# Soft mixture of experts by Strassen products: the left operand of P6 kept in DRAM and used again for P3, and two inner products of seven P3 pairs split once more

## The chip, the cores and the metric

One NeuronCore of a Trainium2 chip runs the whole kernel in one launch. The metric is the device time of the execution in microseconds. The engines are TensorE (PE, with its weight loads PEld beside it), VectorE (DVE), ScalarE (ACT), GpSimd (POOL) and SyncE (SP). SP, ACT and POOL issue DMAs, each on a queue of its own: in the profile q1 carries SP's, q10 ACT's and q0 POOL's.

## What is computed

```python
probs = softmax(router_logits)                 # 16 x 512 tokens, 8 experts
for e in range(n_experts):                     # hidden 512, expert_hidden 2048
    output += probs[:, :, e:e+1] * np.matmul(x, expert_weights[e])
```

The sum over experts is one matrix product: the left operand has a row for each of 8192 tokens and a column for each pair of expert and hidden index (8 x 512 = 4096), with entries prob times x; the right operand is the stack of expert weights, 4096 x 2048.

## The kernel before

**Two levels of Strassen products.** The outer level (Winograd's form, seven products P1 to P7) halves the tokens of a block of 512 into a and b of 256 (16 such blocks, q = 0 to 15), the experts into 0 to 3 and 4 to 7, and the output columns into 1024 and 1024. Each outer product (`Product`, L538) is made by seven inner ones, the steps 1, 5, 6, 2, 7, 3, 4 (`STEPS`, L353), whose operands are halves of 128 tokens, two experts (8 chunks of 128) and 512 columns. A step is 8 matmuls of 128 x 128 by 128 x 512 (`step`, L546); after it `post` (L554) takes sums from PSUM to SBUF with ACT or DVE, and `sink` stores them. Operands are f16.

**Left operands** (`Left`, L443) are two tiles `z` of 128 x 2048, made by DVE in `make`: `times` multiplies the transposed block of x (`xT`) by probabilities spread over partitions (`pT`). With Xa, Xb the blocks and P1, P2, PQ the probabilities of the low experts, of the high ones and their sum, P5 uses Xb PQb; P6 uses `of` minus a product, Z6 = Xb PQb - Xa P1a; P7 and P3 use a difference of two products (`less`), each with a second product in the tile `u`. P3's is Xa PQa - Xb PQb. From a left operand come the difference `d` (step 6) and the sum for steps 3 and 7.

**Right operands** are seven tiles `w` of 1 MB, of 128 x 8 x 512. There are 15 buffers for `w`. P7, P4 and P3 find theirs in DRAM (`wd`) and fetch them on ACT's queue (`fetch_w`, L162; `turnover`, L1064): one tile at every third slot, from the stage before on.

**Stages.** A stage is a pair of products whose steps alternate (`run`, L796), a slot being one step; 14 slots make a pair. The order of stages is: P1 pairs, P2 with P1, P2 pairs, a P5 pair (`k5`), P6 with P5, P6 with P7 (`k7`), P4 with P7, P4 with P3 (`k3`), seven P3 pairs, and P3 of q = 15 alone. The calls registered by `at` run at the beginning of a slot. The lefts of the next stage are queued for DVE after the first slot (L809), the loads of the stage after that are begun there too, or later if `late` says so (L811). DVE's queued work is put between the evacuations by a planned clock of PE and DVE (`slack`, L384), and all engines keep the order in which the program records their instructions.

**The split of P1.** In three P1 pairs, inner products 1 and 5 of both instances are split once more (`by_thirds`, L733). The two instances share the right operand, so that their two left tiles form the two rows of a third 2 x 2 level; the chunks halve into 4 and 4, the columns into 256 and 256. Fourteen groups of 4 matmuls with 256 columns (L764) take the place of four steps of 8 with 512. `Thirds` (L488) makes four sums of the left tiles on DVE, into tiles `h`, and `third_sums` (L178) four sums of a right tile. Partial sums go through ACT copies (L767 to L771, L781) and DVE adds (L774, L777).

**Order on the DMA queues.** SP takes its DMAs in program order, and each waits on SP for what it needs: a buffer's last reader, a store's landing, or the DMA eight places earlier in the joint sequence of SP's and ACT's DMAs, since these share eight semaphores in turn. The same holds for ACT's DMAs, behind which ACT's copies stand. POOL stores results (`out_dram<-h`) and has eight semaphores of its own. SP also loads the sums that P6, P7 and P2 are built upon (`h<-kept`, `h<-out_dram`), and transposes x as it first comes in.

Of the kernel before, what the change touches and what calls it, by code (L numbers as in the profile page):

```python
# [31 lines left out]
def kernel(  # L32
# [41 lines left out]
    def h_tile(shape, dtype):  # L74
        return hpool.tile(shape, dtype, name="h", tag="h")
# [30 lines left out]
    def tt(o, a, b, op):  # L106
        dve(nc.vector.tensor_tensor(out=o, in0=a, in1=b, op=op))  # L107
# [9 lines left out]
    def sp(o, i):  # L117
        note(nc.sync.dma_start(out=o, in_=i))
# [15 lines left out]
    def new_w():  # L134
        return wpool.tile([P, K8, NB], f16, name="w", tag="w")
# [223 lines left out]
    class Task:  # L359


        def __init__(self, cost, make):
            self.cost, self.make, self.done = cost, make, False
# [31 lines left out]

    class XBlock:


        def __init__(self, h, tile_=None):
            self.h, self.t, self.xs, self.new = h, tile_, None, tile_ is not None  # L400
# [21 lines left out]

    class PBlock:


        def __init__(self, h, first, tile_=None):
            self.h, self.first, self.t = h, first, tile_
# [15 lines left out]
    class Left:  # L443


        def __init__(self, xb, pb, less=None, of=None):
            self.xb, self.pb, self.less, self.of = xb, pb, less, of
            self.t, self.task, self.s2, self.i = [None, None], {}, None, None

        def make(self, k):  # L450
            if self.of is not None:
                need(self.of.task[k])
            t = self.t[k] = new_z()
            times(t, k, self.xb, self.pb)
            if self.less is not None:
                u = new_u()
                times(u, k, *self.less)
                tt(t, t, u, SUB)
            if self.of is not None:
                tt(t, self.of.t[k], t, SUB)  # L460

        def queue_make(self, k):
            cost = 1.22 + (2.45 if self.less is not None else 0) + (1.23 if self.of is not None else 0)
            self.task[k] = later(cost, lambda: self.make(k))

        def queue_s2(self):
# [13 lines left out]
        def op(self, p):  # L480
# [4 lines left out]
                    3: (self.i, 0), 7: (self.i, 1)}[p]  # L485
            return t[:, :, ds(i * HP, HP)]

    class Thirds:  # L488


        def __init__(self, a, b):
            self.a, self.b, self.s, self.task = a, b, {}, None

        def make(self):
            e0, e1 = ds(0, C), ds(C, C)
            a, b = self.a.t[0], self.b.t[0]
            for p, x, y, op in ((5, b[:, e0], b[:, e1], ADD), (6, None, a[:, e0], SUB),
                                (3, a[:, e1], None, SUB), (7, a[:, e0], b[:, e0], SUB)):
                o = self.s[p] = h_tile([P, C, HQ], f16)
                x = self.s[5] if x is None else x  # L500
                y = self.s[6] if y is None else y
                tt(o, x, y, op)
# [119 lines left out]


    stages = []
    hooks, late = {}, {}

    def at(stage, slot, make):
        hooks.setdefault((stage, slot), []).append(make)
# [15 lines left out]
    def left_of(r, q, fresh=True):  # L644
        a, b = 2 * q, 2 * q + 1
        if r == 1:
            pt = PBlock(a, P1, xp1[q - 2][1] if q in (2, 3) else None)
            if q in (2, 3):
                xs[a] = XBlock(a, xp1[q - 2][0])
            return Left(xblock(a), pt), [xblock(a), pt]  # L650
        if r in (2, 4):
            h, pt = (a, PBlock(a, P2)) if r == 2 else (b, PBlock(b, P2))
            return Left(xblock(h), pt), [xblock(h), pt]
        if r == 5:
            pt = PBlock(b, PQ)
            return Left(xblock(b), pt), [xblock(b), pt]
        if r == 6:
            pt = PBlock(a, P1)
            return Left(xblock(a), pt, of=lefts[5, q]), [xblock(a), pt]
        pa, pb = PBlock(a, P1 if r == 7 else PQ), PBlock(b, P1 if r == 7 else PQ)  # L660
        return Left(xblock(a), pa, (xblock(b), pb)), [xblock(a), pa, xblock(b), pb]

    def kept_rows(q):
# [43 lines left out]
    def start_loads(stage):  # L707
        if stage < len(stages):
            for p in stages[stage]:
                for load in p.loads:  # L710
                    load.begin()

    def finish_loads(stage):
        if stage < len(stages):
# [18 lines left out]
    def by_thirds(stage):  # L733

        some = stages[stage]
        left = thirds[stage]
        cols = [ds(i * HQ, HQ) for i in range(2)]
        place, keep = {}, {}

        def at_once(what):  # L740
            if what not in place:
                t = place[what] = (bank2 if what[0] == "x" else bank)()
                if what[0] in "gh":
                    some["gh".index(what[0])].banks["x" if what[1] == 1 else "q"] = t
            return place[what]
        slot = 0
        for n, (p, r) in enumerate(((1, 1), (5, 1), (1, 5), (1, 6), (5, 6), (5, 5), (1, 2),
                                    (1, 7), (5, 7), (1, 3), (1, 4), (5, 2), (5, 3), (5, 4))):
            if n in (0, 4, 7, 11):
                for make in hooks.get((stage, slot), ()):  # L750
                    make()
                slot += 1
                if slot == 2:
                    queue_lefts(stage + 1)
                    start_loads(stage + 2)
            x = at_once(("x", p))[:, cols[0]]
            q = at_once("q")[:, cols[p // 5]] if n > 1 else None
            g = at_once(("g", p))
            if r == 1:
                keep[p] = half()  # L760
            o = q if r in (5, 3) else g[:, cols[0]] if r == 2 else x
            z, w = left.op(r, p // 5), third[p][r]
            for c in range(C):
                mm(o, z[:, c, :], w[:, c, :], (r == 1 or (p, r) == (1, 5)) and c == 0, c == C - 1)  # L764
            slack(0.4375, LAG if n < 6 else 1.3)
            if r == 1:
                act(nc.scalar.copy(g[:, cols[0]], x))  # L767
            elif r == 5:
                act(nc.scalar.copy(keep[p][:, cols[1]], q))
            elif r == 6:  # L770
                act(nc.scalar.copy(keep[p][:, cols[0]], x))  # L771
            elif r == 7:
                evacuated(0.42)
                tt(at_once(("h", p))[:, cols[1]], x, keep[p][:, cols[1]], ADD)  # L774
            elif r == 3:
                evacuated(0.42)
                tt(g[:, cols[1]], q, keep[p][:, cols[0]], ADD)  # L777
                if p == 1:
                    some[0].post(1)
            elif r == 4:  # L780
                act(nc.scalar.copy(place["h", p][:, cols[0]], x))  # L781
                if p == 1:
                    some[1].post(1)
        for product in some:
            product.post(5)
        return 4
# [9 lines left out]
    def run(stage):  # L796
        some = stages[stage]
        for p in some:
            p.left.queue_i()
        n = by_thirds(stage) if stage in thirds else 0  # L800
        for i in range(n // 2, len(some[0].steps)):
            for p in some:
                for make in hooks.get((stage, n), ()):
                    make()
                p.step(p.steps[i])
                slack()
                p.post(p.steps[i])
                n += 1
                if n == 1:  # L809
                    queue_lefts(stage + 1)  # L810
                if n == late.get(stage, 1):  # L811
                    start_loads(stage + 2)
                if n == 5:
                    store_loads(stage + 1)
                if n == 7:
                    finish_loads(stage + 2)
# [32 lines left out]
        add(product(3, q), product(3, q + 1))  # L849
    end = add(product(3, 15))  # L850
    late[k3 - 1] = 6
    products[4, 15].apart = True

    def claim(of, tn):
# [142 lines left out]
    def slots_after(stage, slot, n):  # L997
        slot += n
        while slot >= 7 * len(stages[stage]):
            slot -= 7 * len(stages[stage])  # L1000
            stage += 1
        return stage, slot
# [58 lines left out]

    RAW = {1: (0, 0), 2: (1, 0), 3: (1, 1)}

    def turnover(stage, place, r, raw):  # L1064

        right[r].w = {}

        def fetch(p):
            if p in RAW:
                right[r].w[p] = fetch_w(raw, RAW[p])  # L1070
            else:
                right[r].w[p] = fetch_w((r, p), (0, 0))
        at(stage - 1, 9, lambda: fetch(1))
        for i, p in enumerate(STEPS[1:]):
            at(*slots_after(stage, place + 1, 3 * i), lambda p=p: fetch(p))
    turnover(k7 - 1, 1, 7, "t3")
    turnover(k7, 0, 4, "t4")
    turnover(k3 - 1, 1, 3, "b22")


    finish = products[3, 15]
# [32 lines left out]
    finish.step, finish.post = step_at_end, post_at_end  # L1114

    for stage in range(1, ND):
        thirds[stage] = Thirds(*(p.left for p in stages[stage]))
    need_first = [right[1].task[p] for p in (6, 7, 4)]
    for p in (2, 3):
        lefts[1, p].queue_make(0)  # L1120
# [39 lines left out]
```

## Time and profile before

| | |
|---|---|
| median of 3 runs | 1373.86 us (1373.67 to 1374.54) |
| profiled execution: its own time, its span | 1374.01 us, 1372.3 us |
| PE busy in the span | 1365.2 us (99%) |
| DVE, ACT, POOL busy | 1125.6, 190.2, 411.3 us |
| granted clock of TensorE, mean | 0.999 |
| DMA | 338.03 MB, 246 GB/s over the span |
| z<-xT,pT 128x2048, mean of one | 1218 ns |
| stage k5 begins, k7, k3, first P3 pair | about 401, 776, 1163, 1187 us |

The span is the time from the first to the last instruction of the core; the execution has 1.7 us around it. The page lists busy time by engine, then the span in 40 slices, the DMA queues, the chain of work that ended last, and groups of instructions with their mean duration and what ended the idle time before them. Matmuls overlap in the pipeline, so the mean that a group shows for one (378 ns) is longer than the step from one to the next. The trace behind the page answers for any stretch which engine did what, and how long a DMA took from its issue to landing.

### The profile page before, as it was taken

The page shows a single profiled execution, that of the slowest core. Times are in us where ns is not written, and L with a number is a line of the kernel's source. Part 1 is how long each engine was busy: PE and PEld are TensorE (multiplying, and loading weights), DVE is VectorE, ACT ScalarE, POOL GpSimd, SP SyncE. Part 2 cuts the span into 40 slices and gives each one's busy share as a digit, 9 for nine tenths or more (in the row PEclk, how much of TensorE's full clock was granted, in tenths as well). Part 3 has the DMA queues.
Part 4 walks back from the last instruction along what each step waited for, and adds up shares of the span by engine and source line. Part 5 has one row for each costly group of instructions (what it writes and reads, how often), then busy time and mean ns, then how long its engine had stood idle before and what let it go on. Part 6 is the DMA issues. An engine that isn't in the chain of part 4 may idle for free.

```text
span 1372.3 us, 17676 instructions
## 1 busy us (share of the span) xinstructions
PE 1365.2 (99%) x6462; PEld 629.2 (46%) x6462; DVE 1125.6 (82%) x1322; ACT 190.2 (14%) x341; POOL 411.3 (30%) x652
## 2 busy tenths in 40 slices
PE   9999999999999999999999999999999999999998
PEld 4455444444444444444444444444444444444444
DVE  7877767679789888788887988889889898988882
ACT  3332111100011111111111100000000000222221
POOL 3223333331223342334332122333333322232332
PEclk9999999999999999999999999999999999999999
DMA  9998999999898998899897997988898979998786
GB/s 182 231 248 222 212 255 254 243 297 389 239 311 247 297 303 241 268 269 249 243 279 264 335 400 207 235 234 210 227 235 225 244 208 311 254 183 181 167 147 106
DMA packets 191272, 338.03 MB, mean 246 GB/s; under 512 B 52944, under 2 KB 86992, under 8 KB 187472
## 3 DMA queue, kind: packets, MB, share of 16 engines
q0 software_dynamic: 88688, 185.12, 55.9%
q1 hardware_dynamic: 98464, 123.34, 30.5%
q10 hardware_dynamic: 4032, 28.44, 5.3%
q8 instruction: 50, 0.82, 0.2%
q14 instruction: 38, 0.31, 0.1%
HBM read 207.65 MB, written 156.43 MB: 265 GB/s over the span
## 4 chain that ended last, share of the span: by engine, by line
PE 99%; DMA 1%; POOL 0%; issue 0%; ACT 0%; POOLq 0%
PE ps L130 71%; PE pt L130 28%; DMA w<-in_expert_weights_dram 1%; POOL w L121 0%; ACT h L1110 0%; POOL ident L225 0%; POOLq L225 0%; POOLq L1144 0%
## 5 line engine op out<-in xcount | busy, mean ns | idle before, releaser
L130 PEld LDWEIGHTS <-z 128*128 128x128 f16 x5392 | 527.5, 98 | 628.3 <-issue 1.2
L130 PE MATMUL ps<-w,z 128*128 128x512 f16 (+1 forms) x3648 | 804.7, 378 | 0.0
L121 POOL DMA_DIRECT2D out_dram<-h x380 | 248.7, 673 | 745.7 <-ACT h L588 371.2
L130 PE MATMUL pt<-w,z 128*128 128x512 f16 (+1 forms) x1744 | 392.7, 376 | 1.1 <-DMA w<-in_expert_weights_dram 1.1
L107 DVE TENSOR_TENSOR h<-ps,h 128x512 f32<-128x512 f32 x246 | 168.4, 688 | 128.9 <-PE ps L130 122.4
L107 DVE TENSOR_TENSOR z<-xT,pT 128x2048 f16<-128x2048 f16 x220 | 267.0, 1218 | 1.6 <-issue 0.8
L130 PE MATMUL ps<-w,d 128*128 128x512 f16 x880 | 199.1, 379 | 0.0
L107 DVE TENSOR_TENSOR h<-pt,h 128x512 f32<-128x512 f32 x169 | 115.6, 688 | 67.1 <-PE pt L130 62.5
L130 PEld LDWEIGHTS <-d 128*128 128x128 f16 x880 | 86.1, 98 | 103.2
L107 DVE TENSOR_TENSOR z<-z,d 128x2048 f16<-128x2048 f16 x110 | 132.4, 1217 | 0.0
L107 DVE TENSOR_TENSOR w<-w 128x1024 f16<-128x1024 f16 (+2 forms) x100 | 106.1, 1070 | 4.6 <-DMA wd<-w 2.9
L588 ACT COPY h<-ps 128x512 f32<-128x512 f32 x64 | 37.5, 586 | 486.0 <-PE ps L130 457.5
L575 ACT COPY h<-ps 128x512 f32<-128x512 f32 x90 | 52.7, 586 | 373.5 <-PE ps L130 334.5
L107 DVE TENSOR_TENSOR z<-z,u 128x2048 f16<-128x2048 f16 x64 | 78.4, 1225 | 2.2
L107 DVE TENSOR_TENSOR u<-xT,pT 128x2048 f16<-128x2048 f16 x64 | 78.0, 1219 | 0.0
L107 DVE TENSOR_TENSOR d<-z 128x1024 f16<-128x1024 f16 x110 | 75.1, 686 | 1.7
L107 DVE TENSOR_TENSOR ps<-ps,h 128x512 f32<-128x512 f32 (+1 forms) x72 | 48.0, 668 | 15.7 <-PE ps L130 15.2
L121 POOL DMA_DIRECT2D w<-in_expert_weights_dram x65 | 48.9, 784 | 34.0 <-DMA wd<-w 23.3
L121 POOL DMA_DIRECT2D wd<-w x86 | 48.2, 585 | 36.0 <-DVE w L107 25.6
L121 POOL DMA_DIRECT2D kept<-h x56 | 30.8, 550 | 71.4 <-ACT h L575 39.1
L107 DVE TENSOR_TENSOR h<-h 128x512 f32<-128x512 f32 (+2 forms) x69 | 45.1, 676 | 0.1
L567 ACT COPY ps<-ps 128x512 f32<-128x512 f32 x45 | 25.7, 570 | 114.6 <-PE ps L130 107.6
(66 smaller groups left out, 231.9 us busy)
## 6 DMA issues: line engine op xcount, KB each, us to landing
out_dram<-h POOLq DMA_DIRECT2D x380, 256.0 KB, 6.1
pT<-p_dram SPq DMA_DIRECT2D x140, 256.0 KB, 5.9
w<-wd ACTq DMA_DIRECT2D x27, 1024.0 KB, 9.2
h<-kept SPq DMA_DIRECT2D x100, 256.0 KB, 5.8
xT<-x SPq DMA_DIRECT2D x87, 256.0 KB, 5.7
wd<-w POOLq DMA_DIRECT2D x72, 256.0 KB, 5.6
w<-in_expert_weights_dram POOLq DMA_DIRECT2D x35, 512.0 KB, 10.5
h<-out_dram SPq DMA_DIRECT2D x68, 256.0 KB, 5.3
```

The lines of the kernel that those rows point to most:

```text
L107: dve(nc.vector.tensor_tensor(out=o, in0=a, in1=b, op=op))
L121: note(nc.gpsimd.dma_start(out=o, in_=i, **how))
L130: note(nc.tensor.matmul(ps, z, w, start=start, stop=stop, skip_group_check=True))
L567: act(nc.scalar.copy(self.banks["b"], x))
L575: act(nc.scalar.copy(o[TN[p]], b if p == 2 else x))
L588: act(nc.scalar.copy(o[tn], b))
```

## The change

With Xa PQa = Xa P1a + Xa P2a, the left operand of P3 is also Xa P2a - Z6. The change writes both tiles of each Z6 to DRAM (`z_dram`, 16 x 1 MB, two stores of 512 KB on SP per q, in the stage before P6 of that q and at the beginning of its stage), loads it as one tile `w` for P3 (`ZBlock`), and makes P3's left operand by one product and one subtraction (`kept`). The loads of block b for P3 go. The seven P3 pairs are then run by `by_thirds`, with sums of P3's right tiles 1 and 5 (`third3`, made in stage `k3`) and with the sums of left tiles in a buffer of `w` instead of `h` (`room`). P3's weights are fetched at every second slot (`every=2`), all within the stage `k3 - 1` and the first slot of `k3`; in stage `k3` the lefts of the next stage are queued after slot 7 and the loads of the first P3 blocks begin at slot 10, but for the kept tiles of q = 1 and 2, which are loaded at slots 0 and 2.

```diff
-        def __init__(self, xb, pb, less=None, of=None):
+        def __init__(self, xb, pb, less=None, of=None, kept=None):
...
+            if self.kept is not None:
+                tt(t, t, self.kept.t[:, ds(k * K8, K8), :], SUB)
...
+    class ZBlock:
...
+        def begin(self):
+            self.t = new_w().rearrange("p k (two t) -> p (k two) t", two=2)
+            sp(self.t, z_dram[self.q])
...
-        def __init__(self, a, b):
-            self.a, self.b, self.s, self.task = a, b, {}, None
+        def __init__(self, a, b, weights, room=None):
...
+            if self.room is not None:
+                t = self.room().rearrange("p (s c) (two t) -> p s c two t", s=2, two=2)
+                t = {p: t[:, i // 2, :, i % 2] for i, p in enumerate((5, 6, 3, 7))}
...
-        pa, pb = PBlock(a, P1 if r == 7 else PQ), PBlock(b, P1 if r == 7 else PQ)
+        if r == 3:
+            pt, kept_z = PBlock(a, P2), ZBlock(q)
+            return Left(xblock(a), pt, kept=kept_z), [xblock(a), pt, kept_z]
+        pa, pb = PBlock(a, P1), PBlock(b, P1)
...
-                if n == 1:
+                if n == wait_for.get(stage, 1):
                     queue_lefts(stage + 1)
...
+    late[k3] = 10
...
-        at(stage - 1, 9, lambda: fetch(1))
-        for i, p in enumerate(STEPS[1:]):
-            at(*slots_after(stage, place + 1, 3 * i), lambda p=p: fetch(p))
+        if every == 3:
+            at(stage - 1, 9, lambda: fetch(1))
+        for i, p in enumerate(STEPS[every == 3:]):
+            at(*slots_after(stage, place + 1, every * i), lambda p=p: fetch(p))
...
-    turnover(k3 - 1, 1, 3, "b22")
+    turnover(k3 - 1, 1, 3, "b22", 2)
+
+    for q in range(16):
+        z_dram[q] = dram.tile([P, 2 * K8, HQ], f16, name=f"z_{q}")
+
+        def keep_z(k, q=q):
+            sp(z_dram[q][:, ds(k * K8, K8), :], lefts[6, q].t[k])
+        k, half_way = k5 + 1 + q, 7 * len(stages[k5 + q]) * 9 // 14
+        at(k - 1, half_way, lambda keep_z=keep_z: keep_z(0))
+        at(k, 0, lambda keep_z=keep_z: keep_z(1))
...
+    at(k3, 0, load_z(1))
+    at(k3, 2, load_z(2))
...
+    def third_of_p3(p):
+        def make():
+            third3[p] = third_sums(right[3].w[p])
+        later(2.76, make)
+    at(k3, 3, lambda: third_of_p3(1))
+    at(k3, 5, lambda: third_of_p3(5))
+    wait_for[k3] = 7
...
     for stage in range(1, ND):
-        thirds[stage] = Thirds(*(p.left for p in stages[stage]))
+        thirds[stage] = Thirds(*(p.left for p in stages[stage]), third)
+    for stage in range(k3 + 1, end):
+        thirds[stage] = Thirds(*(p.left for p in stages[stage]), third3, new_w)
```

More of the change, by code (lines that the diff above doesn't have):

```diff
@@ L396 @@
     class XBlock:
+        by_hook = False
         def __init__(self, h, tile_=None):
@@ L423 @@
     class PBlock:
+        by_hook = False
         def __init__(self, h, first, tile_=None):
@@ L443 @@
     class Left:
-        def __init__(self, xb, pb, less=None, of=None):
-            self.xb, self.pb, self.less, self.of = xb, pb, less, of
+        def __init__(self, xb, pb, less=None, of=None, kept=None):
+            self.xb, self.pb, self.less, self.of, self.kept = xb, pb, less, of, kept
             self.t, self.task, self.s2, self.i = [None, None], {}, None, None
@@ L460, in make @@
                 tt(t, self.of.t[k], t, SUB)
+            if self.kept is not None:
+                tt(t, t, self.kept.t[:, ds(k * K8, K8), :], SUB)
         def queue_make(self, k):
-            cost = 1.22 + (2.45 if self.less is not None else 0) + (1.23 if self.of is not None else 0)
+            cost = 1.22 + (2.45 if self.less is not None else 0) + (0 if self.of is None and self.kept is None else 1.23)
             self.task[k] = later(cost, lambda: self.make(k))
@@ L486, in op, with __init__, finish @@
             return t[:, :, ds(i * HP, HP)]
+    z_dram = {}
+    class ZBlock:
+        by_hook = False
+        def __init__(self, q):
+            self.q, self.t = q, None
+        def begin(self):
+            self.t = new_w().rearrange("p k (two t) -> p (k two) t", two=2)
+            sp(self.t, z_dram[self.q])
+        def finish(self):
+            pass
+        store = finish
     class Thirds:
-        def __init__(self, a, b):
-            self.a, self.b, self.s, self.task = a, b, {}, None
+        def __init__(self, a, b, weights, room=None):
+            self.a, self.b, self.weights, self.room = a, b, weights, room
+            self.s, self.task = {}, None
         def make(self):
@@ L496, in make @@
             a, b = self.a.t[0], self.b.t[0]
+            if self.room is not None:
+                t = self.room().rearrange("p (s c) (two t) -> p s c two t", s=2, two=2)
+                t = {p: t[:, i // 2, :, i % 2] for i, p in enumerate((5, 6, 3, 7))}
             for p, x, y, op in ((5, b[:, e0], b[:, e1], ADD), (6, None, a[:, e0], SUB),
                                 (3, a[:, e1], None, SUB), (7, a[:, e0], b[:, e0], SUB)):
-                o = self.s[p] = h_tile([P, C, HQ], f16)
+                o = self.s[p] = h_tile([P, C, HQ], f16) if self.room is None else t[p]
                 x = self.s[5] if x is None else x
@@ L624 @@
     stages = []
-    hooks, late = {}, {}
+    hooks, late, wait_for = {}, {}, {}
     def at(stage, slot, make):
@@ L710, in start_loads @@
                 for load in p.loads:
-                    load.begin()
+                    if not load.by_hook:
+                        load.begin()
     def finish_loads(stage):
@@ L761, in by_thirds @@
             o = q if r in (5, 3) else g[:, cols[0]] if r == 2 else x
-            z, w = left.op(r, p // 5), third[p][r]
+            z, w = left.op(r, p // 5), left.weights[p][r]
             for c in range(C):
@@ L1062, with turnover @@
     RAW = {1: (0, 0), 2: (1, 0), 3: (1, 1)}
-    def turnover(stage, place, r, raw):
+    def turnover(stage, place, r, raw, every=3):
         right[r].w = {}
@@ L1072, in fetch, with load_z @@
                 right[r].w[p] = fetch_w((r, p), (0, 0))
-        at(stage - 1, 9, lambda: fetch(1))
-        for i, p in enumerate(STEPS[1:]):
-            at(*slots_after(stage, place + 1, 3 * i), lambda p=p: fetch(p))
+        if every == 3:
+            at(stage - 1, 9, lambda: fetch(1))
+        for i, p in enumerate(STEPS[every == 3:]):
+            at(*slots_after(stage, place + 1, every * i), lambda p=p: fetch(p))
     turnover(k7 - 1, 1, 7, "t3")
     turnover(k7, 0, 4, "t4")
-    turnover(k3 - 1, 1, 3, "b22")
+    turnover(k3 - 1, 1, 3, "b22", 2)
[6 more added lines that the diff above has]
+        at(k, 0, lambda keep_z=keep_z: keep_z(1))
+    def load_z(q):
+        load = products[3, q].loads[-1]
+        load.by_hook = True
+        return load.begin
+    at(k3, 0, load_z(1))
+    at(k3, 2, load_z(2))
+    third3 = {}
+    def third_of_p3(p):
[5 more added lines that the diff above has]
+    wait_for[k3] = 7
     finish = products[3, 15]
```

## The prediction, made before the result was known

> **What bounds the kernel now.** I read the page first: the busy times and the chain that ended last.
>
> ```profile
> PE 1365.2 (99%) x6462; PEld 629.2 (46%) x6462; DVE 1125.6 (82%) x1322; ACT 190.2 (14%) x341; POOL 411.3 (30%) x652
> ...
> PE 99%; DMA 1%; POOL 0%; issue 0%; ACT 0%; POOLq 0%
> PE ps L130 71%; PE pt L130 28%; DMA w<-in_expert_weights_dram 1%; POOL w L121 0%; ACT h L1110 0%; POOL ident L225 0%; POOLq L225 0%; POOLq L1144 0%
> ```
>
> The chain is PE from end to end, so a matmul less is time won, if nothing else starts to make PE wait. Next come the timelines of PE in a stage that is already split (P1) and in a P3 pair, with start, length and count.
>
> ```profile
> 65.33 1.04 PE L130 MATMUL pt<-w,z 128*128 128x256 f16 x8
> ...
> 71.44 3.62 PE L130 MATMUL ps<-w,d 128*128 128x512 f16 x16
> ...
> 88.71 1.04 PE L130 MATMUL pt<-w,z 128*128 128x256 f16 x8
> ```
> ```profile
> 1218.08 3.62 PE L130 MATMUL ps<-w,d 128*128 128x512 f16 x16
> ...
> 1242.26 3.62 PE L130 MATMUL ps<-w,d 128*128 128x512 f16 x16
> ```
>
> A split P1 stage lasts 88.71 - 65.33 = 23.38 us, of which its 56 matmuls of 256 columns take 71.44 - 65.33 = 6.11 us (109 ns each). A P3 pair, from its step 6 to the next one's, lasts 24.18 us: 112 matmuls of 512 columns at 215.9 ns.
>
> Last, who is near to stopping PE. The stage windows give stretch and length, then PE, PEld, DVE, ACT and POOL busy, clock, DMA share, GB/s.
>
> ```profile
> 88.90:112.30 23.40, 23.40 (x138) 13.30 (x137) 15.11 (x20) 8.24 (x19) 6.93 (x12) 1.00 1.08 263
> 1235.40:1259.60 24.20, 24.20 (x114) 10.96 (x113) 20.43 (x21) 5.83 (x10) 6.90 (x9) 1.00 0.80 178
> 776.20:800.30 24.10, 24.10 (x114) 10.93 (x112) 21.11 (x26) 1.76 (x3) 4.32 (x8) 1.00 1.03 383
> ```
>
> The third is the stage that changes from P6 to P7 (k7). The waits of PE's weight loads name one weight tile from DRAM there, and the timelines of PEld and ACT with the DMA issues in two windows (784 to 785 and 772.4 to 777) say how it comes about.
>
> ```profile
> 798.42 8.38 PEld L130 LDWEIGHTS <-z 128*128 128x128 f16 x40 [0.25 <-DMA w<-wd]
> ```
> ```profile
> 782.82 0.58 ACT L575 COPY h<-ps 128x512 f32<-128x512 f32 x1 [16.34 <-DMA out_dram<-h]
> 784.91 0.33 ACTq L164 DMA_DIRECT2D w<-wd  x1
> ```
> ```profile
> w<-wd ACTq DMA_DIRECT2D x1, 1024.0 KB, 13.5
> h<-out_dram SPq DMA_DIRECT2D x1, 256.0 KB, 8.2
> ```
>
> ACT stood for 16 us behind a store, then issued weight loads. The one issued at 784.91 landed 13.5 us later, at 798.4, exactly when step 4 of the first P7 product began. It could not be issued sooner: 784.85 is when the load of h that SP issued at 776.65 landed (8.2 us), and the two share a semaphore of the ring of eight. PE lost nothing, with nothing to spare.
>
> **The change part by part.** *Matmuls.* Seven stages trade 32 matmuls of 512 for 56 of 256. The operands and banks are those of P1's split, so the P1 stage is the price: 24.18 - 23.38 = 0.80 us each, 7 x 0.80 = **5.6 us gained**.
>
> *DVE in a P3 pair.* A left operand loses one product and keeps one subtraction, now against the kept tile. After the change a pair has 4 products (1.218), 4 subtractions (1.225, the row z<-z,u), 2 d (0.686), 2 z<-z,d (1.217), 4 third sums (0.69, the rows h<-z and h<-h,z), 4 adds of 256 (0.433) and 4 of 512 (0.688): 4.87 + 4.90 + 1.37 + 2.43 + 2.76 + 1.73 + 2.75 = 20.8 us of 23.38 (89%; before 20.4 of 24.2). It fits; what counts is whether DVE is free for the adds that PE waits for inside the split. In P1 the first add started 3.74 us into the stage (92.45) and PE did not stop. Walking through the changed order with these durations, I get 3.65 us in later stages and about 3.7 in the second, the tightest. Cost 0; if one 1.2 us operation slips in front, up to 0.9 us a stage. ACT goes to about P1's 8.2 us of 23.4.
>
> *Entry to P3 (k3).* Weights of P3 are fetched at every second slot instead of every third. In the changed order each is issued about 13 slots, 22 us, ahead of its step; a 1 MB load there took 7.8 to 9.6 us, and 16.6 at worst anywhere near k7. Cost 0. The kept tiles of q = 1 and 2 are the late ones: SP may issue them at 1162.8 and 1164.5, when their buffers come free. At 9 us they land by 1173.5; at 14.9, the slowest load before ACT's block at k7, by 1179.4. DVE, after 8 third sums of the weights (5.5 us), needs the second at about 1178, and the add queued behind it frees a bank that PE asks for near 1183. Cost 0, up to 2 us if the load takes over 18. That the lefts of the first pair are queued at slot 7 and not 1 takes DVE to about 23 of 24.2 us there (22.9 before).
>
> *Loads in P3.* A pair loses 4 loads of 256 KB and gains 2 of 1 MB, asked for more than a stage ahead, where DMA moved 123 to 205 GB/s. Cost 0.
>
> *Stores in P6.* Sixteen times 2 x 512 KB on SP, behind the transposes and ahead of the next xT and pT loads. DVE has made both halves 3 to 8 us before SP gets there (its transposes start at 647.7 and 665.7 in two of these stages), so SP hardly waits; behind it stand loads that DVE uses a stage later. P6 moved 271 GB/s; 1.05 MB more per 24.2 us makes 314. P1 stages at a DMA share of 1.08 to 1.18 and k7 at 383 GB/s ran without a PE wait; in P6 POOL waited up to 7.5 us and DVE once 2.9 us for stores of parts, and PE lost nothing. Cost 0; without that cover, where landings go from 5.8 to k7's 9 us, perhaps 3 us in all.
>
> *The last two stores (q = 15).* SP issues them at about 772.4 and 777.7, between the two h loads. From 766 to 832 DMA's share is never under 0.98 but for one us: everything asked for there waits its turn. They put 1.05 MB ahead of the tile with nothing to spare; the second now holds its semaphore slot. At the 0.41 MB/us of that stretch this is 2.5 us. From 780 to 782, though, DMA moved only 0.19 MB/us, and 2 x (0.41 - 0.19) = 0.44 MB may fit in, which leaves 0.61 MB or 1.5 us. Below that lies nothing (0, if what the stores delay is other work); above, the store's landing decides (last rival). I take the middle, **2.0 us lost**. Later weight tiles shift as PE does: those issued at 785.98 and 802.58 had 4 and 2 us to spare.
>
> By the Trainium skill, DMA: Bandwidth & Descriptors, section Queues, rings and completion order, each engine takes a packet from each queue in turn, which would slow ACT's store from 772 on and give the 2.5. The trace has 31, 32 and 32 packets of the three queues from 796 to 797, in accord, but 2 of SP's against 37 and 35 from 773 to 774 with a load outstanding, which speaks for the 1.5.
>
> **Sum.** The profiled execution took 1374.0 us (span 1372.3 and 1.7 around it), 0.15 above the median of the runs, which is no difference here. 1374.0 - 5.6 + 2.0 = **1370.4 us**, 0.26% less. About 0.2%, 2.7 us, is what a measurement can tell from no change.
>
> **The rivals.** *Turnover covered:* the two stores displace only work with slack. For it: SP's h loads and the stores also move. Against: the full stretch. 1374.0 - 5.6 = 1368.4.
>
> *The gain is half eaten:* the stall is 3 to 5 us, or DVE comes late for the split's adds (0.4 us x 7), or the kept tile at k3 does. For it: 89% DVE. Against: the walk above. About 1372, between 1371.3 and 1374.
>
> *Slower:* the semaphore of the q = 15 store. The weight tile may not be issued before it has landed. If that takes as long as the h loads issued at 787 did (15.5 us), it lands at 777.7 + 15.5 = 793.2, and 13.5 us more is 806.7, 8.3 us late: 1374.0 - 5.6 + 8.3 = 1376.7. It decides from a landing of 12.8 us on (5.6 us late). Against: 8.2 to 10.9 us for SP's loads of those microseconds.
>
> *A matmul of 256 columns costs more than 4/7 of one of 512* (123 ns): then the split loses. The P1 row has 109 ns, with weight loads of 98 ns inside, so I give it 0.01; at 150 ns it would be 7 x (8.4 - 6.9) = 10 us slower, 1384. The Trainium skill, TensorE: Matmul & The Clock Gate, section Back-to-back issue gap, gives sustained figures of about 81 ns at 128 columns and 131 at 512, by which (an estimate, 98 ns at 256) 56 would cost 5.5 us against 4.2; the trace's 109 and 216 ns differ, and the measurement decides. That the split is not done at all is excluded: the changed program has 168 more matmuls, 7 x 24.
>
> **How the numbers follow.** Forecast 0.45; covered 0.25; half eaten 0.16; slower 0.13; matmul 0.01. Faster by over 0.2%: the covered case and nine tenths of the forecast, 0.66. Slower by over 0.2%: the last two in part, 0.11, and other small waits of the same kind, 0.02: 0.13. The rest, 0.21, is within. The range, 1368.0 to 1373.6, takes in the covered case and most of the half eaten one.
>
> **What would show it.** P3 pairs of 23.4 us between their steps 6, with PE busy throughout; the wait of PEld for a tile from DRAM near 798 grown from 0.25 to about 2 us and PE idle as long; no wait of PE for DVE in P3; no PE wait from 438 to 770. Wrong, if PE waits elsewhere, if the wait at 798 is as small as before, or if a P3 pair takes over 23.6 us.

## The result, and the profile after

The changed kernel takes 1382.6 us (median of 6 runs, 1379.6 to 1386.0) against 1374.3 us before: ratio 1.0061, 95% interval 1.0044 to 1.0079. It is **slower**. The profiled execution took 1381.43 us, its span is 1379.7 us.

The page of the changed kernel, busy times and chain that ended last:

```profile
PE 1362.8 (99%) x6630; PEld 645.9 (47%) x6630; DVE 1121.1 (81%) x1354; ACT 206.8 (15%) x397; POOL 411.6 (30%) x652
...
PE 64%; issue 15%; DMA 14%; POOL 6%; DVE 1%; POOLq 0%; ACT 0%; SPq 0%; DVEq 0%; ACTq 0%
```

Busy shares hardly moved, but the chain is no longer PE alone: a third of it is DMAs and the engines that wait for them. First the gain. PE's timeline in the changed P3 (start, length, operation, count):

```profile
1223.34 1.04 PE L130 MATMUL pt<-w,z 128*128 128x256 f16 x8
...
1229.45 3.62 PE L130 MATMUL ps<-w,d 128*128 128x512 f16 x16
...
1246.72 1.04 PE L130 MATMUL pt<-w,z 128*128 128x256 f16 x8
```

1246.72 - 1223.34 = 23.38 us a pair, as forecast, without a wait of PE. The first pair, however, begins at 1199.96 instead of 1187.0. Everything is lost before it, in two places. PE's timeline again, only rows with idle time (in brackets, with what ended it), first of P6, then of the turnover k7:

```profile
589.18 3.61 PE L130 MATMUL pt<-w,z 128*128 128x512 f16 x16 [1.49 <-DVE h L107]
595.13 5.30 PE L130 MATMUL ps<-w,d 128*128 128x512 f16 x16 [2.33 <-DVE ps L107]
...
809.51 5.36 PE L130 MATMUL ps<-w,z 128*128 128x512 f16 x24 [2.90 <-DMA w<-wd]
...
827.88 1.89 PE L130 MATMUL ps<-w,z 128*128 128x512 f16 x8 [0.93 <-DVE h L107]
...
833.90 7.08 PE L130 MATMUL ps<-w,z 128*128 128x512 f16 x32 [0.68 <-DMA w<-wd]
```

With two more (1.89 us at 573.73, 0.55 at 718.39), P6 loses 6.3 us in waits and k7 4.5. The row at 595.13 holds a third loss: its 16 matmuls took 5.30 us instead of 3.62. Stretches of 2 us there (stretch, length, then PE, PEld, DVE, ACT, POOL busy, granted clock, DMA share, GB/s):

```profile
596.00:598.00 2.00, 2.00 (x7) 0.75 (x6) 1.97 (x3) 0.00 (x0) 0.57 (x1) 0.62 1.04 407
598.00:600.00 2.00, 2.00 (x6) 0.75 (x5) 2.00 (x4) 0.00 (x0) 0.00 (x0) 0.53 1.08 251
600.00:602.00 2.00, 2.00 (x11) 0.88 (x10) 2.00 (x3) 0.58 (x1) 1.38 (x3) 1.00 0.55 112
```

After standing for 3.8 of the 7.4 us before 595.1, PE ran for nearly 4 us at about half clock, which adds 1.7 us. In sum 6.3 + 1.7 + 4.5 = 12.5 us lost; from the spans it is 1379.7 - (1372.3 - 5.6) = 13.0.

*How P6 stalls.* PE waits for DVE, so the next question is what DVE waits for. Its timeline:

```profile
578.99 0.68 DVE L107 TENSOR_TENSOR h<-ps,h 128x512 f32<-128x512 f32 x1
587.11 1.42 DVE L107 TENSOR_TENSOR w<-w 128x1024 f16<-128x1024 f16 x2 [7.44 <-DMA wd<-w]
```

The operation at 587.11 is an in-place sum on a part of P4's weights (`sums_in_place`); it overwrites what POOL was still storing. DVE takes its work in order, so the evacuations behind it were 7.4 us late, and PE ran out of free banks. Before, the same wait was 2.9 us and cost nothing:

```profile
579.58 1.42 DVE L107 TENSOR_TENSOR w<-w 128x1024 f16<-128x1024 f16 x2 [2.86 <-DMA wd<-w]
```

What came between, by the timelines of SP and of POOL's issues in the changed kernel:

```profile
576.73 0.88 SPq L118 DMA_DIRECT2D z<-z  x2
```
```profile
577.57 1.14 POOL L121 DMA_DIRECT2D wd<-w  x2 [4.28 <-DVE w L107]
```

SP, held up by transposes, issued both stores of one Z6 (1 MB) just ahead of POOL's stores of the part.

*How k7 stalls.* The chain of the changed kernel there, in order of time:

```profile
784.79 14.33 DMA z<-z
799.12 0.02 issue
799.14 0.02 ACTq L164
799.16 0.04 issue
799.20 10.27 DMA w<-wd
809.46 0.05 issue
809.51 5.36 PE ps L130 x24
```

The second store of q = 15 took 14.33 us; the weight tile that shares its semaphore was issued at 799.2, landed 10.3 us later, and PE started at 809.51. That is the mechanism of the rival "slower".

### The profile page after: what moved, and what is told of

The parts are those of the page before. It is cut to its first block, busy times and chain, and to the rows that moved or that the text cites. A ratio compares the mean times of both kernels' runs of the same rounds, so it can differ in the third digit from the quotient of the medians.

```text
span 1379.7 us, 18165 instructions
## 1 busy us (share of the span) xinstructions
PE 1362.8 (99%) x6630; PEld 645.9 (47%) x6630; DVE 1121.1 (81%) x1354; ACT 206.8 (15%) x397; POOL 411.6 (30%) x652
## 4 chain that ended last, share of the span: by engine, by line
PE 64%; issue 15%; DMA 14%; POOL 6%; DVE 1%; POOLq 0%; ACT 0%; SPq 0%; DVEq 0%; ACTq 0%
PE ps L130 48%; PE pt L130 16%; DMA wd<-w 5%; POOL out_dram L121 3%; DMA w<-in_expert_weights_dram 3%; DMA out_dram<-h 3%; DMA w<-wd 2%; POOL w L121 1%; DMA z<-z 1%; POOL wd L121 1%; POOL xs L121 0%; DVE z L107 0%; DVE h L107 0%; POOLq L121 0%; DVE w L107 0%
## 5 line engine op out<-in xcount | busy, mean ns | idle before, releaser
L130 PEld LDWEIGHTS <-z 128*128 128x128 f16 x5336 | 521.8, 98 | 613.8 <-issue 6.1
L130 PE MATMUL pt<-w,z 128*128 128x512 f16 (+1 forms) x1632 | 357.8, 369 | 2.0 <-DVE h L107 1.5
L107 DVE TENSOR_TENSOR h<-ps,h 128x512 f32<-128x512 f32 x260 | 177.0, 687 | 115.2 <-PE ps L130 101.4
L107 DVE TENSOR_TENSOR h<-pt,h 128x512 f32<-128x512 f32 x155 | 105.6, 687 | 52.2 <-PE pt L130 46.3
L107 DVE TENSOR_TENSOR w<-w 128x1024 f16<-128x1024 f16 (+2 forms) x108 | 111.5, 1041 | 22.6 <-DMA wd<-w 12.9
L614 ACT COPY h<-ps 128x512 f32<-128x512 f32 x64 | 37.4, 586 | 491.7 <-PE ps L130 426.0
L601 ACT COPY h<-ps 128x512 f32<-128x512 f32 x90 | 52.7, 586 | 374.9 <-PE ps L130 343.9
L107 DVE TENSOR_TENSOR ps<-ps,h 128x512 f32<-128x512 f32 (+1 forms) x86 | 54.0, 629 | 20.8 <-PE ps L130 16.5
L597 ACT COPY h<-ps 128x512 f32<-128x512 f32 x65 | 36.4, 601 | 79.7 <-PE ps L130 72.8
L107 DVE TENSOR_TENSOR z<-z,w 128x2048 f16<-128x2048 f16 x32 | 39.2, 1225 | 1.7 <-DMA w<-z 0.7
```

Of the source, the lines that this page charges most:

```text
L130: note(nc.tensor.matmul(ps, z, w, start=start, stop=stop, skip_group_check=True))
L597: act(nc.scalar.copy(o[tn], q if p == 5 else x))
L601: act(nc.scalar.copy(o[TN[p]], b if p == 2 else x))
L614: act(nc.scalar.copy(o[tn], b))
```

## The experiments

Theory A: the bytes of the stores make P6's DMAs late (DVE stands, PE follows), and the stores of q = 15 hold the weight tile at k7. Theory B: the stores' place among SP's DMAs and on the shared semaphores does it, whatever their size. Theory C: the use of Z6 in P3 costs part. Each kernel was timed beside the kernel before on one chip; the median of the kernel before was 1373.5 to 1373.9 us beside them. The kernels of rows 1, 4 and 8 use the stored Z6 of one block for all; they leave out a right P3 of the others.

| kernel | us, median (lowest to highest) | ratio to before, 95% interval |
|---|---|---|
| all stores but those of q = 0 left out | 1368.03 (1367.5 to 1368.7) | 0.9955, 0.994 to 0.997 |
| before + all stores | 1388.01 (1387.9 to 1389.6) | 1.0101, 1.0086 to 1.0117 |
| no stores of q = 0, 15 (version 3) | 1375.29 (1370.1 to 1379.0) | 1.0006, 0.9994 to 1.0017 |
| all stores, an eighth of the bytes | 1372.07 (1370.0 to 1376.4) | 0.9987, 0.9977 to 0.9997 |
| three split pairs | 1370.98 (1370.2 to 1372.1) | 0.9983, 0.9974 to 0.9991 |
| parts' sums later | 1374.48 (1369.1 to 1379.9) | 1.0004, 0.9990 to 1.0018 |
| stores taken apart | 1371.88 (1369.4 to 1375.0) | 0.9988, 0.9980 to 0.9997 |
| version 3, half of the bytes | 1367.86 (1367.7 to 1368.6) | 0.9960, 0.9947 to 0.9972 |
| five split pairs | 1370.94 (1368.5 to 1377.6) | 0.9983, 0.9971 to 0.9994 |
| five pairs, stores apart | 1370.77 (1369.8 to 1371.6) | 0.9976, 0.9967 to 0.9985 |
| before + stores of q = 15 | 1382.11 (1381.2 to 1383.3) | 1.0061, 1.0049 to 1.0073 |
| the same, k7's loads late | 1378.84 (1377.1 to 1380.4) | 1.0033, 1.0021 to 1.0045 |
| five pairs, k7's loads late | 1374.84 (1372.1 to 1378.8) | 1.0008, 0.9999 to 1.0017 |
| stores apart, k7's loads late | 1376.21 (1370.1 to 1384.5) | 1.0016, 0.9999 to 1.0034 |

**1. The change without its stores.**

```diff
-            sp(self.t, z_dram[self.q])
+            sp(self.t, z_dram[0])
...
-    for q in range(16):
+    for q in range(1):
```

> Left out: the stores of Z6 for q = 1 to 15; every left operand of P3 is made with the stored Z6 of q = 0, so 15 of 16 blocks get a wrong P3. The split, its sums, the loads of the kept tiles and the entry to P3 stay. Theory A (the stores' bytes delay what P6 and k7 wait for; the split itself is worth its 5.6 us): 1374.3 - 5.6 = 1368.7 us, no wait of PE between 430 and 1180. Theory B (the stores' place among SP's DMAs and on the shared semaphores does the harm, not their bytes): 1368.7 as well. Theory C (the use in P3 or the entry to it costs part of it): above 1371, with waits of PE after 1160.

1368.03 us, with no wait of PE after the first 60 us. The split and its entry to P3 gain 5.5 us and cost nothing else: theory C falls.

**2. The stores without the change.** The kernel before with the stores' loop of the change, nothing else.

> The kernel before, unsplit, with the 32 stores of Z6 added where the changed kernel has them; nothing reads them, the output is complete. Theories A and B: the waits of the changed kernel without its gain, 1374.3 + 12.9 = 1387 us. Theory C: 1374 to 1378.

1388.01 us, 14.4 more than before. The two halves add up: -5.5 + 14.4 = +8.9, against +8.3 for the change.

**3. No stores of q = 0 and 15**, called version 3 below.

```diff
-        if r == 3:
+        if r == 3 and 0 < q < 15:
...
-    for q in range(16):
+    for q in range(1, 15):
```

> The changed kernel without the stores of q = 0 and q = 15, whose P3 lefts are made from two products as before (neither is in a split pair, so all seven splits stay; the output is complete). If the wait at k7 comes from the stores of q = 15 (theories A and B): its 2.9 + 0.9 + 0.7 us go and the waits in P6 stay, 1382.6 - 4.5 = 1378 us. If other DMA work fills that stretch anyway: 1382.

1375.29 us, 6.6 better than the changed kernel when each is set against before (+1.7 and +8.3 us): more than the 4.5 expected. In its profile k7 has no wait; P6 has 5.9 us of them, now from 645 to 675 and not at 573 to 596, and 1.7 us of slow matmuls behind the last. How much P6 loses is not fixed either: the same program took 1370 us in one run and 1379 in another.

**4. All stores, an eighth of the bytes.**

```diff
-            sp(z_dram[q][:, ds(k * K8, K8), :], lefts[6, q].t[k])
+            n = K8 if q == 0 else 1
+            sp(z_dram[q][:, ds(k * K8, n), :], lefts[6, q].t[k][:, 0:n])
```

> All 32 stores stay in number and place, but for q over 0 each writes only its first chunk, 64 KB of 512 KB; every left operand of P3 is made with the stored Z6 of q = 0, so 15 of 16 blocks get a wrong P3. Theory A (bytes): an eighth of the 12.9 us or less is left, 1368.7 to 1370.5 us. Theory B (place in SP's order and on the semaphores): near the changed kernel, 1380 to 1383.

1372.07 us, between the two: both theories hold, each in one place. PE's timeline has no wait in P6, and at k7:

```profile
808.83 3.68 PE L130 MATMUL ps<-w,d 128*128 128x512 f16 x16 [2.55 <-DMA w<-wd]
...
819.40 1.89 PE L130 MATMUL ps<-w,z 128*128 128x512 f16 x8 [1.72 <-DVE h L107]
```

So P6's loss is one of bytes, and k7's is mostly one of order: with two stores of 64 KB in that place PE still waits 4.3 us, of the 6.6 that experiment 3 took away. That these two move which DMA waits for which is argued from the order of the DMAs, not tested by itself.

**5. Half of the bytes**, on version 3 (`n = C`, half of each store, for q over 1; all loads from the stored Z6 of q = 1).

> The version without q = 0 and 15, but for q over 1 each store writes half of its 512 KB; every split pair uses the stored Z6 of q = 1, so P3 is wrong in 13 blocks. A dose between none (1368.0) and all (1375.3). In proportion to the bytes: 1371.7. If there is a threshold, as the eighth without any wait in P6 suggests (waits once DMA is full): 1368 to 1370.

1367.86 us, as without stores, so the loss is not in proportion to the bytes: it begins between half of them and all. Where it begins is not sharp: with the stores of ten blocks (five pairs, experiment 6) one program took 1368.5 us in one run and 1377.6 in another. The stretch from 438 to 776 us before, with half of the bytes, with all (version 3), and with ten blocks; the last two columns are DMA share and GB/s:

```profile
437.80:776.20 338.40, 338.40 (x1569) 153.43 (x1568) 287.77 (x357) 48.42 (x83) 113.04 (x201) 1.00 0.91 271
```
```profile
437.80:776.20 338.40, 338.40 (x1569) 153.43 (x1568) 287.83 (x357) 48.49 (x83) 112.87 (x201) 1.00 1.00 293
```
```profile
437.80:776.20 338.40, 332.40 (x1530) 149.93 (x1529) 279.33 (x347) 48.40 (x83) 109.86 (x196) 0.99 1.05 304
```
```profile
437.80:776.20 338.40, 338.40 (x1570) 153.38 (x1569) 287.58 (x358) 48.44 (x83) 112.56 (x200) 1.00 1.00 302
```

GB/s does not tell where the loss begins. Ten blocks moved 302 without a wait of PE. Version 3 shows only 304 because its P6 ends 7.5 us later, so that the window holds less of it; the same bytes went at 311 in the profile of experiment 7. The share tells more, but it is no ceiling: it can go over 1, and the first two changed P3 pairs run at 1.07 and 1.08 without a wait. In the kept profiles PE waits in P6 wherever the share of this stretch is 1.02 or more, and nowhere at 1.00 or less. Part of that is the jam itself, for one program is on both sides: five pairs, 1.00 here, and 1.02 at 293 GB/s with 4.6 us of waits in experiment 9.

What grows with the bytes is the time to landing. That of SP's loads `h<-kept`, issued from 540 to 730 us, without stores, with half and with all:

```profile
h<-kept SPq DMA_DIRECT2D x31, 256.0 KB, 7.1
```
```profile
h<-kept SPq DMA_DIRECT2D x31, 256.0 KB, 9.0
```
```profile
h<-kept SPq DMA_DIRECT2D x29, 256.0 KB, 11.4
```

Two microseconds more were covered, four were not: DVE's waits for DMAs in P6 sum to 2.9 us before, 4.3 with half and 23.5 with all. These times, too, differ between executions: in the short one of experiment 7, with all bytes, the loads took 7.9 us and the waits sum to 12.4.

**6. Where the bytes fall: three and five pairs, and the two stores apart.** The stores and the splits are kept for some pairs only, the other P3 lefts being made from two products; the cuts here and in 7 are against version 3.

```diff
-        if r == 3 and 0 < q < 15:
+        if r == 3 and q in KEEP:
...
-    for stage in range(k3 + 1, end):
+    for stage in (k3 + 1, k3 + 2, k3 + 7):
```

> Stores only for q = 1 to 4, 13 and 14, and only the P3 pairs (1,2), (3,4) and (13,14) are split; the others keep their two products. Output complete. Theory A now (in P6 the bytes collide with the parts of P4's weights, which POOL casts, DVE sums and POOL stores from about 548 to 725 us; a store outside that stretch costs nothing): three gains of 0.80, 1373.6 - 2.4 = 1371.2 us and no wait of PE in P6. Rival D (any megabyte added to P6 costs its share, 10 us over 14 blocks, 0.7 us each): 6 x 0.7 - 2.4 = 1.8 slower, 1375.4.

> Stores for q = 1 to 4, 7, 8 and 11 to 14 only; the P3 pairs (5,6) and (9,10) stay unsplit with two products. Output complete. In the stretch of P4's parts (548 to 725 us) this leaves a store in about half of the stages, as many bytes there as the half dose that cost nothing. Threshold: 1373.5 - 5 x 0.80 = 1369.5 us. If a whole megabyte in single stages is enough to fill DMA: one or two waits of 2 to 3 us, 1371 to 1374.

Three pairs, with no store while P4's parts are made: 1370.98, 2.6 us less than before, no wait of PE from 370 to 910. The price per megabyte (rival D) falls. Five pairs: 1370.94, not 1369.5. The profiled execution (1369.2 us) has no wait of PE after the first 60 us; others took up to 1377.6.

> The version without q = 0 and 15, with each pair of stores taken apart: the first ahead of the transposes (slot 6 of the stage before), the second at slot 3 of its own stage, so that SP no longer issues both at once. Same bytes, output complete. If the burst of 1 MB within a microsecond is what hurts: 1369 to 1371.5 us against 1375.3. If it is the sum of bytes in the stage: 1374 to 1377.

```diff
-        at(k - 1, half_way, lambda keep_z=keep_z: keep_z(0))
-        at(k, 0, lambda keep_z=keep_z: keep_z(1))
+        at(k - 1, 6 if half_way == 9 else half_way, lambda keep_z=keep_z: keep_z(0))
+        at(k, 3, lambda keep_z=keep_z: keep_z(1))
```

> The same five pairs, with the two stores of a block taken apart (slot 6 of the stage before, slot 3 of its own). If both thinning and spreading help: 1369.5 us with a narrower spread than without. If thinning alone is enough: the same as the version with five pairs and stores together. If the later second store comes into the way of the loads there: 1371 to 1373.

Apart, with seven pairs: 1371.88 against 1375.29, so that the burst makes about half of the loss. Its profile (1374.74 us, one of its longer executions) has 3.2 us of waits in P6, and at k7, without any store of q = 15, one of 2.46 us for a weight tile, behind which 24 matmuls took 7.04 us instead of 5.34. With five pairs: 1370.77, with 1.8 us between the lowest and the highest run instead of 9, and a wait of 1.6 us at k7 that keeps it from 1369.5. This version is the best complete one tried: faster than both kernels, 0.24% than before (0.15 to 0.33), though not to be told from three or five pairs with the stores together.

**7. The parts' sums later** (version 3).

```diff
-    by_parts(*slots_after(k5 + 2, 4, 60), 24, 4, load_p4, less_t2, (8, 15))
+    by_parts(*slots_after(k5 + 2, 4, 60), 24, 4, load_p4, less_t2, (11, 20))
```

> The version without q = 0 and 15, with the sums on the parts of P4's weights put off: the difference at slot 11 of 24 instead of 8, the in-place sums at slot 20 instead of 15. All bytes and splits stay, output complete. If it is DVE's standing behind loads and stores of those parts that stops PE: most of the waits go, 1368.4 to 1371 us against 1375.3. If DVE then stands as long behind the loads of h, or bytes delay something else: 1374 to 1377.

1374.48 us: no difference that can be told from 1375.29. The kept profile is of one of its shorter executions (1370.0 us; the runs go from 1369.1 to 1379.9). In it DVE's wait for the stores of parts is 1.1 us in all, against 5.8 in version 3, and DVE still stands for the sums of P6 (`h<-kept` 4.9 us) and for stores of results (`out_dram<-h` 4.0); PE waits once, 2.3 us. So the wait of 7.4 us that I read in the profile is one of several, and putting its sums later does not move the median. What the longer executions wait for is not shown.

**8. The stores of q = 15 alone**, added to the kernel before.

> The kernel before with only the two stores of q = 15 added, at the end of P6; nothing reads them, output complete. If these two cost what PE waited at k7 in the changed kernel (2.9 + 0.9 + 0.7 us; 4.3 with small stores): 1373.5 + 4.4 = 1377.9 us. By the 2.0 us of the prediction: 1375.5. If the wait there needs the delay that the earlier stores leave behind: 1373.5 to 1374.5.

1382.11 us, **8.2 us for 1 MB**; none of the three expectations. PE's timeline:

```profile
801.22 8.13 PE L130 MATMUL ps<-w,z 128*128 128x512 f16 x24 [3.25 <-DMA w<-wd]
809.19 3.62 PE L130 MATMUL pt<-w,z 128*128 128x512 f16 x16
813.39 3.62 PE L130 MATMUL ps<-w,d 128*128 128x512 f16 x16 [0.59 <-DMA w<-wd]
...
823.91 1.89 PE L130 MATMUL ps<-w,z 128*128 128x512 f16 x8 [1.72 <-DVE h L107]
```

The store issued at 776.00 took 12.0 us. The weight tile behind it was issued at 788.03 instead of 784.91, 3.1 us later, and landed after 13.1 us; with nothing to spare, PE waits 3.25. Then the 24 matmuls take 8.13 us where they took 5.36 in the changed kernel; the granted clock was 0.50 to 0.53 from 801 to 807. With 0.59 and 1.72 us more this makes 3.25 + 2.77 + 0.59 + 1.72 = 8.3 us. The last wait comes, in this run, by another branch of the queue: a load of x that SP issued at 777.49 took 17.3 us, the sums behind it 15.9, and DVE, which stood 12.2 us for them, worked without a gap from there to what PE waited for.

**9. The loads of k7 begun later**: one line, `late[k7] = 12`.

> The kernel before with the two stores of q = 15 alone (1382.1 us), and the loads of x and probabilities for the stage after next begun at slot 12 of stage k7 instead of slot 1, so that the four loads of sums stand ahead of them on SP. Same bytes, output complete. If PE's loss comes from the full queue of SP and ACT behind the store (loads of x that took 17 us, sums behind them): 1374 to 1377 us. If the weight tile that waits for the store's landing sets it by itself: the wait of 3.3 us and the slow matmuls behind it stay, 1379 to 1382.

> Five split pairs, stores together, no stores of q = 0 and 15 (1370.9 us, from 1368.5 to 1377.6), and the same later loads at k7. Output complete. If k7 is where its slow executions lose time: near 1369.5 us with a narrower spread. If P6 is: no change, 1371.

> All seven split pairs, stores of q = 1 to 14 taken apart (1371.9 us, where PE waited 2.5 us at k7 and 3.1 in P6), and the same later loads at k7. Output complete. If the k7 part goes: 1369 to 1370 us. If it doesn't: 1372.

With q = 15 alone: 1378.84, from +8.2 to +5.2 us. DVE's wait of 12.2 us for the sums fell to 0.4, but both waits of PE stayed:

```profile
800.79 5.35 PE L130 MATMUL ps<-w,z 128*128 128x512 f16 x24 [2.60 <-DMA w<-wd]
...
820.21 3.33 PE L130 MATMUL ps<-w,z 128*128 128x512 f16 x8 [1.98 <-DVE h L107]
```

Behind the second, DVE now stood 4.2 us for stores of results instead, one of which took 15.2 us, and 8 matmuls took 3.33 us instead of 1.89. So the sums alone do not make that wait: with a DMA share of 1.01 to 1.03 there, stores took their place. The two profiles differ by 2.0 us, and most of what was gained is the slow stretch behind the first wait: 24 matmuls in 5.35 us instead of 8.13.

On the two versions without the stores of q = 15 the same line made things worse (+3.9 and +4.3 us); both expectations failed. It brings a wait for a weight tile to k7 (1.1 us, then 0.9 for DVE) where the profile with five pairs had none: moving DMAs there can change which one another waits for, as the small stores did. Part of it is not the edit's: the program is the same up to 776 us, and PE waited 4.6 us in P6 in this profiled execution, none in the other. That the rest of the medians' difference comes from k7 is likely, not shown; the versions with and without the line also ran on different chips.

## Why the prediction was wrong, step by step

The forecast was 1370.4 us, the measured time 1382.6. The gain came as forecast; the two terms for the stores did not.

- **Matmuls, 5.6 us gained:** right. 5.5 us without the stores; 23.38 us a pair.
- **DVE in a P3 pair, entry to P3, loads in P3, cost 0:** right. No wait of PE in P3 or at its entry; DVE was busy 20.7 us a pair in the mean of six, against the 20.8 of the sum.
- **"Stores in P6 ... Cost 0": this is the step that failed.** Fourteen blocks cost 1375.29 - 1368.03 = 7.3 us. I took the head-room from GB/s: 271 plus 1.05 MB a stage "makes 314", and k7 ran at 383 without a wait. The runs showed that the rate is no limit by itself (302 without a wait, 304 and 311 with some). The DMAs that DVE waits for landed later: in the profile of version 3 the loads of sums took 11.4 us instead of 7.1, DVE stood 23.5 us for DMAs instead of 2.9, and behind it PE lost 5.9 us in waits and 1.7 in slow matmuls. That P1 stages at a share of 1.08 ran without a wait shows only that nothing in them stood near its limit. In P6, with POOL waiting up to 7.5 us and DVE once 2.9 for stores, something did, and I read those waits as cover rather than as the distance to the edge. My own "without that cover ... perhaps 3 us in all" was also too small, since a stall costs clock besides.
- **The last two stores, 2.0 us:** the place was right, the size was not: 8.2 us when alone, about 6.6 within the change (with those of q = 0). I weighed the two stores as bytes (1.5 to 2.5 us). Experiment 4 shows that order does most of it: an eighth of the bytes left 4.3 us of waits. The rival "slower", the semaphore of the q = 15 store, had the mechanism, and nearly its price (8.3 us) by another sum: it wanted a landing of 15.5 us and all loss in one wait, where 12.0 us were enough for a wait of 3.25 and the rest came from the clock (2.77), from one more tile (0.59) and from DVE, late behind other DMAs (1.72). "It decides from a landing of 12.8 us on" was therefore wrong. One reading of that stretch was too flat: by single microseconds its DMA share is below 0.98 in eight of the 66, down to 0.82, though over stretches of 10 us it is 1.01 to 1.03, as the price supposed.
- **"No PE wait from 438 to 770"** was the test that I named for being wrong, and it is the one that failed.

The sum as measured: -5.5 + 7.3 + 6.6 = +8.4 us; the change, +8.3. These terms are differences along one row of kernels and must add up. An independent pair does so less well: 7.3 + 8.2 = 15.5 us for the fourteen blocks and q = 15 alone, against the 14.4 of all stores without the split.

## What to carry to other kernels

Before adding DMA traffic to a stage, do not take its head-room from GB/s. Look at the DMA share (0.91 here left room for half of what looked like a small addition) and above all at who in the stage already waits for DMAs: beyond that point the added bytes became landing time for all others. Where a trace shows a load that arrives just in time, a DMA put into the same sequence of semaphores can be dear whatever its size; leave those out first (here two blocks' stores, that no split needed). A dose (none, an eighth, half, all) tells bytes from order with one edit. Where runs of one program scatter by 9 us, one profile explains one execution and not the median.

## What the runs showed of the hardware

PE's granted clock fell to about a half after it had stood: 0.53 to 0.62 for 4 us after waits of 1.49 and 2.33 us, and 0.50 to 0.53 for 6 us after one of 3.25, with the weight loads of matmuls of 512 columns 0.427 us apart. A single wait of 2.46 us (stores taken apart, 0.50 from 805 to 807) or 2.75 (version 3, 0.50 from 676 to 678) was enough too; after the wait of 2.90 us at 809.51 in the changed kernel, no slow matmuls followed. So a stall of 3 us can cost 6 (3.25 + 2.77). The Trainium skill, TensorE: Matmul & The Clock Gate, section What's actually happening, says that the array falls to half its clock after an idle window of some 3.4 us that runs freely, and comes back after a busy one. The slow rate agrees (426.7 ns cold in its next section), but the waits of 2.46 and 2.75 us are shorter than such a window, so that here less than a whole idle one was enough. That the window runs freely would explain why one wait was followed by it and another was not, which no run here can show.
